# Attention in fp32: the first quarter of the softmax weights split into two parts like the rest, and a new order for GpSimd's low parts

## The chip, the cores and the metric

The kernel runs on one core of a Trainium2 chip. The metric is the time of the whole program in microseconds of device time, as the median over runs. The core has five engines that work through queues of their own: TensorE (PE) for matrix products, with its weight loads (PEld), VectorE (DVE), ScalarE (ACT), GpSimd (POOL) and SyncE (SP), which issues most of the transfers.

## The reference

One layer of an encoder with 2048 positions and 1024 channels, all in float32: a normalization, one input projection, differential attention with four heads, a recurrent group, an output projection and a gated feed-forward network. The change lies in the attention alone:

```python
def block(start):
    qb = lax.dynamic_slice_in_dim(qh, start, Q_BLOCK, axis=1)
    sc = jnp.einsum('bqhcd,bkhcd->bhcqk', qb, kh).astype(jnp.float32) * scale
    dist = jnp.abs(start + jnp.arange(Q_BLOCK)[:, None] - key_pos[None, :]).astype(jnp.float32)
    sc = sc - slopes[:, None, None, None] * dist
    p = jax.nn.softmax(sc, axis=-1)
    w = p[:, :, 0] - lam * p[:, :, 1]
    return jnp.einsum('bhqk,bkhe->bqhe', w, vh)
```

Each head has two score maps (`c` = 0 and 1, of 64 channels each). Their softmaxes are combined into one weight matrix `w` (`lam` is a number learned), and `w` is multiplied by the values. Then each head's output is normalized (`rms_norm(o, subln_g)`).

## The kernel before

The program has four phases, one after the other: input projections and recurrent group, attention (`phase2`), output projection with its normalization, feed-forward network. A product in fp32 is made in one of two ways. Either PE multiplies fp32 operands directly, or both operands are split into a high part (rounded to fp32r) and a low part (what is left, in fp32r), and `mm3` (L80 to L83) adds up three passes: high by high, high by low, low by high.

The attention goes through 64 query tiles of 128 rows (four heads of 16), one to a `step(n, cur)`. Two tiles of a head form a `Pair`, whose products with the values are made together (256 columns). The steps are a pipeline: step n makes the scores of tile n, and in the same step finishes the softmax of tile n-1 (`b1`), transposes the weights of tile n-2 (`b2`), splits the second half of the weights of tile n-3 (`b3`), and multiplies the weights of an older pair by the values (`pv`). Normalization of the outputs follows two and four steps later (`nrm`, `fin`). PE, DVE, ACT and POOL issue exactly in the order in which `step` is written; the tile framework adds the waits. What a tile goes through:

- `scores(hf)`: PE makes half a row of scores (1024 keys) for both maps, into PSUM tiles `sc`, which have two buffers.
- `biased(c, hf)`: DVE adds the distance bias (`strip`) and keeps the running minimum `mn`; the sum goes to SBUF tiles `e` (L453).
- `softmax(c)`: ACT takes the exponential of the 2048 entries of one map (L458), map 0 at the end of step n and map 1 at the beginning of step n+1.
- `ratio`, `combine(hf)`: DVE makes the factor of the second map (L464, L465) and adds the second map times the factor to the first, in two halves (L469). These are the combinations; all their operands are in SBUF.
- `transposed(i)`, i = 0 to 3: PE transposes a quarter of the 2048 columns into a PSUM tile `tp` (two buffers, L475), and ACT copies it to SBUF (L484): quarter 0 into `wTn`, quarter 1 into `wf` (one buffer), quarters 2 and 3 into the halves of `wg` (two buffers).
- `parts(1)`, `parts(2)`: ACT rounds `wf` (and `wg`) to the high part `wTh` (L75) and POOL subtracts that for the low part `wTl` (L78). Those of `wg` are made a step later than its copies.
- `values(part)`: PE multiplies a quarter of the weights by the values. Quarters 1 to 3 go through `mm3`. Quarter 0 is one fp32 product of `wTn` with `vn` (L507), the sum of the two parts of the values, which POOL makes once a head (L416).
- In the step in which a pair's last quarter is done, ACT copies the output to `o` (L514). POOL has small work for its normalization: `osq`, `s` in one step, `rr`, `rb` (twice) in the next.

In `step` the order around the change is:

```python
if b2:
    b2.transposed(0)
    b2.transposed(1)
    b2.parts(1)
if b3:
    b3.parts(2)
```

and behind it values, `ratio` and `combine(0)` of `b1`, the second half of the scores and of the biased sums, `transposed(2)` and `transposed(3)`, softmax 0, more values, and `combine(1)`.

Of the kernel before, what the change touches and what calls it, by code (L numbers as in the profile page):

```python
# [9 lines left out]
F32 = mybir.dt.float32  # L10
F32R = mybir.dt.float32r
F16 = mybir.dt.float16
BF16 = mybir.dt.bfloat16
AF = mybir.ActivationFunctionType
ALU = mybir.AluOpType
# [3 lines left out]
P = 128  # L19
# [3 lines left out]
NT = S // P  # L23
NH = 4
# [18 lines left out]
def encoder_layer(ctx, tc, x, w_qkr, w_v, w_out, w_up, w_down, w_a, w_x, par, lams, g_attn, g_ffn, g_fin, out):  # L43
# [3 lines left out]
    def pool_of(name, **kw):  # L47
        return tc.tile_pool(name=name, reuse_waits="tile", **kw)
# [314 lines left out]
    def phase2(kp):  # L363
        es = ExitStack()
# [3 lines left out]
        qp = es.enter_context(pool_of("aq", bufs=2))  # L368
        lop = es.enter_context(pool_of("al", bufs=2))
        tp_ = es.enter_context(pool_of("at", bufs=2))  # L370
        vp = es.enter_context(pool_of("av", bufs=2))
        ep = es.enter_context(pool_of("ae", bufs=2))
        pre = es.enter_context(pool_of("apre", bufs=1))
        ps_s = es.enter_context(pool_of("ps_s", bufs=2, space=PSUM))
        ps_t = es.enter_context(pool_of("ps_t", bufs=2, space=PSUM))
        ps_v = es.enter_context(pool_of("ps_v", bufs=1, space=PSUM))
        PQ = 2 * P
        NQ = 1

        ones = cp.tile([P, P], F32, name="ones")  # L380
        V.memset(ones, 1.0)
# [28 lines left out]
        def load_values(h, vs):  # L410
            for vt, src in zip(vs, v_d):
                nc.sync.dma_start(vt.bitcast(F32), src[:, h])

        def sum_values(vs):
            vn = vp.tile([P, 4 * NQ, P], F32, name="vn", tag="vn")
            G.tensor_tensor(out=vn, in0=vs[0][:, 0:4 * NQ, :].bitcast(F32), in1=vs[1][:, 0:4 * NQ, :].bitcast(F32), op=ALU.add)  # L416
            vs.append(vn)

        def load_q(h, g):
            qs = []  # L420
# [6 lines left out]
        class Tile:  # L427
# [38 lines left out]

            def combine(self, hf):
                e0, e1 = [e[:, hf * 1024:(hf + 1) * 1024] for e in self.e]
                V.scalar_tensor_tensor(out=e0, in0=e1, scalar=self.rc, in1=e0, op0=ALU.mult, op1=ALU.add)  # L469

            def transposed(self, i):

                tp = ps_t.tile([P, 4, P], F32, name="tp", tag="tp")
                for m in range(4):
                    T.transpose(tp[:, m, :], self.e[0][:, (4 * i + m) * P:(4 * i + m + 1) * P], ident)  # L475
                if i == 0:
                    dst = self.pair.wn[:, :, self.t % 2 * P:(self.t % 2 + 1) * P]
                elif i == 1:
                    dst = self.wf = tp_.tile([P, 4, P], F32, name="wf", tag="wf", bufs=1)
                else:  # L480
                    if i == 2:
                        self.wg = tp_.tile([P, 8, P], F32, name="wg", tag="wg")
                    dst = self.wg[:, (i - 2) * 4:(i - 1) * 4, :]
                A.activation(out=dst, in_=tp, func=AF.Copy)  # L484

            def parts(self, i):

                j = self.t % 2
                dst = (slice(None), slice(0, 4) if i == 1 else slice(4, 12), slice(j * P, (j + 1) * P))
                split(self.pair.wh[dst], self.pair.wl[dst], self.wf if i == 1 else self.wg, lo_eng=G)  # L490

        class Pair:


            def __init__(self, h, u, vs):
                self.h, self.u, self.vs = h, u, vs
                self.s0 = sm.tile([P, 2], F32, name="s0", tag="s0", bufs=8)
                self.wn = hip.tile([P, 4 * NQ, PQ], F32, name="wTn", tag="wTn")
                self.wh = hip.tile([P, NT - 4 * NQ, PQ], F32R, name="wTh", tag="wTh")
                self.wl = lop.tile([P, NT - 4 * NQ, PQ], F32R, name="wTl", tag="wTl")  # L500

            def values(self, part):
                if part == 0:
                    self.pv = ps_v.tile([P, PQ], F32, name="pv", tag="pv")
                for kt in range(part * 4, part * 4 + 4):
                    if part < NQ:
                        T.matmul(self.pv, self.vs[2][:, kt, :], self.wn[:, kt, :], start=kt == 0, stop=False)  # L507
                    else:
                        m = kt - 4 * NQ
                        mm3(self.pv, self.vs[0][:, kt, :], self.vs[1][:, kt, :], self.wh[:, m, :], self.wl[:, m, :],  # L510
                            kt == 0, kt == NT - 1)
                if part == 3:
                    self.o = sm.tile([P, PQ], F32, name="o", tag="o", bufs=3)
                    A.activation(out=self.o, in_=self.pv, func=AF.Copy)  # L514
                    self.sq = sm.tile([P, PQ], F32, name="osq", tag="osq", bufs=1)
                    G.tensor_tensor(out=self.sq, in0=self.o, in1=self.o, op=ALU.mult)
                    self.s2 = sm.tile([P, 2], F32, name="s2", tag="s2")
                    G.tensor_tensor(out=self.s2, in0=self.s0, in1=self.s0, op=ALU.mult)
# [73 lines left out]
        def step(n, cur):  # L592

            b1 = tiles[n - 1] if 0 <= n - 1 < last else None
            b2 = tiles[n - 2] if 0 <= n - 2 < last else None
            pair = lambda lag: pairs[(n - lag) // 2] if n >= lag and (n - lag) // 2 < len(pairs) else None
            pv, nrm, fin = pair(4), pair(6), pair(8)
            if n % 2:
                nrm = fin = None
            b3 = tiles[n - 3] if 0 <= n - 3 < last else None  # L600
            if cur:
                cur.scores(0, n < 3)
            if n < 3:
                keep_clock(nrm_ps[:, 0:P], 3)
            if b1:
                b1.softmax(1)
            if cur:
                cur.biased(0, 0)
                cur.biased(1, 0)
            if b2:  # L610
                b2.transposed(0)
                b2.transposed(1)
                b2.parts(1)
            if b3:
                b3.parts(2)
            if pv:
                pv.values(n % 2 * 2)
            if fin:
                fin.norm_spread()
            if b1:  # L620
                b1.ratio()
                b1.combine(0)
            if cur:
                cur.scores(1, n < 3)
                if n < 3:
                    keep_clock(nrm_ps[:, 0:P], 3)
                cur.biased(0, 1)
                cur.biased(1, 1)
            if b2:
                b2.transposed(2)  # L630
                b2.transposed(3)
            if cur:
                cur.softmax(0)
            if pv:
                pv.values(n % 2 * 2 + 1)
            if nrm:
                nrm.norm_sums()
            if b1:
                b1.combine(1)
            if fin:  # L640
                fin.scaled()
            if nrm:
                nrm.norm_scale()

        ordered = {mybir.EngineType.PE, mybir.EngineType.DVE, mybir.EngineType.Activation, mybir.EngineType.Pool}
        ks, vs = load_head(0, [slice(0, D)])
# [7 lines left out]
        qs_next = load_q(0, 0)  # L654
        load_keys(0, ks, [slice(D, S)])
        load_values(0, vs)
        sum_values(vs)
        n = 0
        manual = ExitStack()
        manual.enter_context(tc.manual_schedule(engines=ordered))  # L660
# [1 line left out]
        for h in range(NH):  # L662
            for t in range(NT):
# [6 lines left out]
                if t % 4 == 1:  # L670
                    if t + 4 < NT:
                        qs_next = load_q(h, t // 4 + 1)
                    elif h + 1 < NH:
                        nxt = load_head(h + 1, [slice(0, S)])
                        qs_next = load_q(h + 1, 0)
                        load_values(h + 1, nxt[1])
                if t == NT - 1 and h + 1 < NH:
                    sum_values(nxt[1])
                if h == NH - 1 and t in (6, 8, 10, 12):
                    raw = fetch_out(t // 2 + 1)  # L680
                if h == NH - 1 and t in (7, 9, 11, 13):
# [823 lines left out]
```

## Time and profile before

| | us |
|---|---|
| median of three runs | 2653.01 (2652.57 to 2661.96) |
| the profiled execution, its own time | 2648.49 |
| its span, first to last instruction | 2646.7 |
| PE busy | 2583.5 (98%) |
| DVE busy | 1976.1 (75%) |
| ACT busy | 1341.9 (51%) |
| POOL busy | 586.3 (22%) |

The shares are over the whole span. Attention is one phase of four, so its limits are read from windows inside it and from the timeline of a step, not from these shares. The ends of PE's matrix products are modelled, so that PE may look busy while it waits; waits are better read from the idle times in brackets at the ends of timeline rows.

### The profile page before, as it was taken

To read this page: it belongs to the slowest core of one execution; us is meant where nothing else is said; L and a number is where in the kernel's file an instruction comes from. 1 tells how busy PE (TensorE), PEld (TensorE's weight loads), DVE (VectorE), ACT (ScalarE), POOL (GpSimd) and SP (SyncE) were. 2 spreads that over 40 slices of the span, in tenths; PEclk is the share of its full clock that TensorE was granted. 3 is DMA by queue.
4 is the path that set the end of the run, shared out by engine and by line. 5 is a ranking of instruction groups with operands and counts; after the bars stand their busy time and mean duration, and the time that the engine had idled before them with its cause. 6 is when DMAs were issued, how large, how long until landed. Compare 5 with 4: busy or idle time off the path is not lost. (4 is left out here: it accounts for less than half of the span.)

```text
span 2646.7 us, 33694 instructions
## 1 busy us (share of the span) xinstructions
PE 2583.5 (98%) x13018; PEld 2107.9 (80%) x13018; DVE 1976.1 (75%) x2487; ACT 1341.9 (51%) x1732; POOL 586.3 (22%) x488
## 2 busy tenths in 40 slices
PE   9999999999999999999999999989999999999998
PEld 7878778778888888787778888878888887778786
DVE  5454554699999999644488888898888777675776
ACT  4343542688888888632344444454444443332433
POOL 0113313346667676700000000000000000111100
PEclk9999999999999999999999999999999999999999
DMA  6421221321202001344443343454665344755743
GB/s 192 132 88 58 82 80 64 133 93 34 72 23 88 25 25 39 99 152 136 173 158 131 131 147 120 151 162 157 242 227 203 128 147 116 210 121 131 233 148 128
DMA packets 146018, 329.36 MB, mean 124 GB/s; under 512 B 18624, under 2 KB 74688, under 8 KB 137024
## 3 DMA queue, kind: packets, MB, share of 16 engines
q1 hardware_dynamic: 133632, 283.82, 31.1%
q0 software_dynamic: 11504, 41.42, 6.4%
q8 instruction: 102, 1.67, 0.3%
q10 hardware_dynamic: 720, 1.95, 0.2%
q14 instruction: 60, 0.49, 0.1%
HBM read 198.16 MB, written 128.97 MB: 124 GB/s over the span
## 5 line engine op out<-in xcount | busy, mean ns | idle before, releaser
L1003 ACT ACTIVATE wg<-sw 128x1024 fp32r<-128x1024 f32 (+1 forms) x136 | 140.7, 1034 | 399.3 <-PE q L1029 220.6
L1044 DVE TENSOR_TENSOR u<-q,u 128x512 f32<-128x512 f32 x340 | 234.3, 689 | 138.8 <-PE q L1029 134.9
L458 ACT ACTIVATE e<-e,mn 128x2048 f32<-128x2048 f32 x128 | 256.2, 2007 | 11.3 <-DVE mn L453 11.3
L449 PE MATMUL sc<-ks,qt 64*128 64x512 f32 x1536 | 228.2, 410 | 6.2 <-DVE mn L453 6.0
L1189 DVE SCALAR_TENSOR_TENSOR acc<-u,prm,acc 128x1023 f32<-128x1023 f32 (+1 forms) x176 | 225.9, 1284 | 8.5 <-ACT acc L1181 4.0
L469 DVE SCALAR_TENSOR_TENSOR e<-e,rc,e 128x1024 f32<-128x1024 f32 x128 | 211.1, 1650 | 2.3
L83 PE MATMUL ps<-hT_hi,wl 128*128 128x512 f32 x512 | 199.6, 390 | 0.0
L82 PE MATMUL ps<-hT_lo,wh 128*128 128x512 f32 x512 | 199.6, 390 | 0.0
L81 PE MATMUL ps<-hT_hi,wh 128*128 128x512 f32 x512 | 199.4, 390 | 0.0
L449 PEld LDWEIGHTS sc<-ks,qt 64*128 64x128 f32 x1536 | 147.5, 184 | 45.2 <-DVE mn L453 9.3
L1008 DVE TENSOR_TENSOR wg<-sw,wg 128x1024 fp32r<-128x1024 f32 (+1 forms) x136 | 161.7, 1189 | 28.0 <-ACT wg L1003 28.0
L1008 DVE TENSOR_TENSOR wg<-wr,wg 128x512 fp32r<-128x512 f32 (+3 forms) x136 | 126.8, 932 | 68.3 <-ACT wg L1003 68.3
L1003 ACT ACTIVATE wg<-wr 128x512 fp32r<-128x512 f32 (+3 forms) x136 | 111.7, 822 | 118.9 <-PE q L1029 104.9
L453 DVE CUSTOM_DVE_ANT_0 e<-sc,strip,mn 128x1024 f32<-128x1024 f32 x128 | 159.1, 1280 | 14.2 <-PE sc L449 13.3
L1294 POOL DMA_DIRECT2D b15f<-in_w_down_dram x1 | 0.8, 814 | 705.0 <-DVE u L1102 705.0
L78 POOL TENSOR_TENSOR wTl<-wg,wTh 128x1024 fp32r<-128x1024 f32 x64 | 156.5, 2446 | 0.0
L453 DVE CUSTOM_DVE_ANT_0 e<-sc,strip 128x1024 f32<-128x1024 f32 x128 | 150.8, 1213 | 5.0 <-PE sc L449 5.0
L1029 PE MATMUL q<-b0r,wg 128*128 128x512 f32 x448 | 152.7, 398 | 0.0
L1029 PE MATMUL q<-b14r,wg 128*128 128x512 f32 x440 | 149.4, 397 | 2.9 <-ACT u L1051 2.9
L78 POOL TENSOR_TENSOR wTl<-wf,wTh 128x512 fp32r<-128x512 f32 x64 | 126.7, 1980 | 110.1 <-ACT wTh L75 107.4
L1029 PE MATMUL q<-b12r,wg 128*128 128x512 f32 x440 | 149.4, 397 | 0.0
L475 PEld LDWEIGHTS tp<-ident,e 128*128 128x128 f32 x1024 | 110.6, 141 | 45.2 <-ACT wTh L75 18.7
(320 smaller groups left out, 6669.6 us busy)
## 6 DMA issues: line engine op xcount, KB each, us to landing
wr<-in_w_up_dram SPq DMA_DIRECT2D x66, 512.0 KB, 5.5
s_d<-sw SPq DMA_DIRECT2D x22, 1024.0 KB, 4.7
sw<-s_d SPq DMA_DIRECT2D x22, 1024.0 KB, 4.8
a_d<-acc SPq DMA_DIRECT2D x154, 128.0 KB, 1.9
x_d<-u POOLq DMA_DIRECT2D x32, 512.0 KB, 5.4
wr<-a_d SPq DMA_DIRECT2D x32, 512.0 KB, 4.8
xt<-in_x_dram SPq DMA_DIRECT2D x30, 512.0 KB, 4.6
ws<-in_w_qkr_dram SPq DMA_DIRECT2D x16, 512.0 KB, 3.3
```

The lines of the kernel that those rows point to most:

```text
L78: lo_eng.tensor_tensor(out=lo, in0=src, in1=hi, op=ALU.subtract)
L82: T.matmul(ps, lh, rl, start=False, stop=False)
L83: T.matmul(ps, ll, rh, start=False, stop=last)
L449: T.matmul(self.sc[c][:, n * CH:(n + 1) * CH], l[rows, q], r[rows, kk], start=i == 0, stop=i == 2)
L453: V.tensor_tensor_reduce(out=self.e[c][:, hf * 1024:(hf + 1) * 1024], in0=self.sc[c], in1=strip[:, off:off + 1024], scale=SLOPES[self.h], ...
L458: A.activation(out=self.e[c], in_=self.e[c], func=AF.Exp, scale=-1.0, bias=self.mn[:, 2 * c + 1:2 * c + 2], accum_out=self.s[c])
L469: V.scalar_tensor_tensor(out=e0, in0=e1, scalar=self.rc, in1=e0, op0=ALU.mult, op1=ALU.add)
L1003: A.activation(out=hi, in_=src, func=AF.Copy)
L1008: V.tensor_tensor(out=lo, in0=src, in1=hi, op=ALU.subtract)
L1029: T.matmul(ps, l, r[:, k, :], start=new is not None and k == 0 and n == 0, stop=k == m - 1 and n == 2, skip_group_check=True)
L1044: V.tensor_tensor(out=out, in0=a, in1=b_, op=ALU.add)
L1189: V.scalar_tensor_tensor(out=acc[:, 0:n], in0=u[:, o + tap:o + tap + n], scalar=prm[:, C_FW + 3 * m + tap:C_FW + 3 * m + tap + 1], in1=acc ...
```

## The change

The first quarter is now treated like the others. `transposed(0)` no longer copies `tp`: ACT rounds it from PSUM into the high part, and DVE subtracts that from PSUM for the low part. `wTh` and `wTl` hold all 16 blocks of keys, `wTn`, `vn` and `sum_values` are gone, and `values` always uses `mm3`. The tile `wg` has one buffer in place of two. In `step`, `parts(2)` of `b3` now stands ahead of `parts(1)` of `b2`, which moved behind `combine(0)`. Two dependencies are added by hand: POOL's low part of `wg` waits for the `combine(1)` of the step before, its low part of `wf` for the `combine(0)` of the same step.

```diff
             def combine(self, hf):
                 e0, e1 = [e[:, hf * 1024:(hf + 1) * 1024] for e in self.e]
-                V.scalar_tensor_tensor(out=e0, in0=e1, scalar=self.rc, in1=e0, op0=ALU.mult, op1=ALU.add)
+                return V.scalar_tensor_tensor(out=e0, in0=e1, scalar=self.rc, in1=e0, op0=ALU.mult, op1=ALU.add)
...
                 if i == 0:
-                    dst = self.pair.wn[:, :, self.t % 2 * P:(self.t % 2 + 1) * P]
+
+                    o = (slice(None), slice(0, 4), slice(self.t % 2 * P, (self.t % 2 + 1) * P))
+                    A.activation(out=self.pair.wh[o], in_=tp, func=AF.Copy)
+                    V.tensor_tensor(out=self.pair.wl[o], in0=tp, in1=self.pair.wh[o], op=ALU.subtract)
+                    return
                 elif i == 1:
                     dst = self.wf = tp_.tile([P, 4, P], F32, name="wf", tag="wf", bufs=1)
                 else:
                     if i == 2:
-                        self.wg = tp_.tile([P, 8, P], F32, name="wg", tag="wg")
+                        self.wg = tp_.tile([P, 8, P], F32, name="wg", tag="wg", bufs=1)
                     dst = self.wg[:, (i - 2) * 4:(i - 1) * 4, :]
                 A.activation(out=dst, in_=tp, func=AF.Copy)
 
             def parts(self, i):
 
                 j = self.t % 2
-                dst = (slice(None), slice(0, 4) if i == 1 else slice(4, 12), slice(j * P, (j + 1) * P))
-                split(self.pair.wh[dst], self.pair.wl[dst], self.wf if i == 1 else self.wg, lo_eng=G)
+                dst = (slice(None), slice(4, 8) if i == 1 else slice(8, 16), slice(j * P, (j + 1) * P))
+                src = self.wf if i == 1 else self.wg
+                A.activation(out=self.pair.wh[dst], in_=src, func=AF.Copy)
+                return G.tensor_tensor(out=self.pair.wl[dst], in0=src, in1=self.pair.wh[dst], op=ALU.subtract)
...
                 for kt in range(part * 4, part * 4 + 4):
-                    if part < NQ:
-                        T.matmul(self.pv, self.vs[2][:, kt, :], self.wn[:, kt, :], start=kt == 0, stop=False)
-                    else:
-                        m = kt - 4 * NQ
-                        mm3(self.pv, self.vs[0][:, kt, :], self.vs[1][:, kt, :], self.wh[:, m, :], self.wl[:, m, :],
-                            kt == 0, kt == NT - 1)
+                    mm3(self.pv, self.vs[0][:, kt, :], self.vs[1][:, kt, :], self.wh[:, kt, :], self.wl[:, kt, :],
+                        kt == 0, kt == NT - 1)
...
             if b2:
                 b2.transposed(0)
                 b2.transposed(1)
-                b2.parts(1)
             if b3:
-                b3.parts(2)
+                after(b3.parts(2), "second")
...
             if b1:
                 b1.ratio()
-                b1.combine(0)
+                marks["first"] = b1.combine(0)
+            if b2:
+                after(b2.parts(1), "first")
...
             if b1:
-                b1.combine(1)
+                marks["second"] = b1.combine(1)
...
+        def after(ins, mark):
+
+            if mark in marks:
+                tc.add_manual_dep(ins.ins, marks[mark].ins.name,
+                                  mybir.DependencyInfo(mybir.DependencyClass.Sync, mybir.DependencyReason.SCHED_ONLY),
+                                  reason="shared access to SBUF")
```

On ACT, a step from the middle of the attention stood so before; a number in a name is that of a tile, `wg_7757` and `wg_7865` are the `wg` of two tiles that follow each other, and `tp` are the transposes:

```order
L484 ACTIVATE wTn_7470<-tp_7811 128x4x128
L484 ACTIVATE wf_7822<-tp_7817 128x512
L75 ACTIVATE wTh_7471<-wf_7822 128x4x128
L75 ACTIVATE wTh_7471<-wg_7757 128x8x128
L484 ACTIVATE wg_7865<-tp_7860 128x512
L484 ACTIVATE wg_7865<-tp_7867 128x512
```

A step of the change on ACT, between the same neighbours:

```order
L472 ACTIVATE wTh_7605<-tp_7963 128x4x128
L481 ACTIVATE wf_7975<-tp_7970 128x512
L488 ACTIVATE wTh_7605<-wg_7909 128x8x128
L488 ACTIVATE wTh_7605<-wf_7975 128x4x128
L481 ACTIVATE wg_8018<-tp_8013 128x512
L481 ACTIVATE wg_8018<-tp_8020 128x512
```

The first copy became a high part, and the high part of `wg` moved ahead of that of `wf`. The copies into the next `wg` stand behind both, as before.

On POOL, two steps of the attention before, the second with the small work `rr` and `rb`:

```order
L78 TENSOR_TENSOR wTl_5130<-wf_5478,wTh_5129 128x4x128
L78 TENSOR_TENSOR wTl_5130<-wg_5413,wTh_5129 128x8x128
L516 TENSOR_TENSOR osq_5544<-o_5542 128x256
L518 TENSOR_TENSOR s2_5546<-s0_4905 128x2
L78 TENSOR_TENSOR wTl_5342<-wf_5589,wTh_5341 128x4x128
L78 TENSOR_TENSOR wTl_5130<-wg_5521,wTh_5129 128x8x128
```

and of the change:

```order
L489 TENSOR_TENSOR wTl_5169<-wg_5468,wTh_5168 128x8x128
L489 TENSOR_TENSOR wTl_5169<-wf_5534,wTh_5168 128x4x128
L510 TENSOR_TENSOR osq_5600<-o_5598 128x256
L512 TENSOR_TENSOR s2_5602<-s0_4936 128x2
L489 TENSOR_TENSOR wTl_5169<-wg_5577,wTh_5168 128x8x128
L489 TENSOR_TENSOR wTl_5388<-wf_5645,wTh_5387 128x4x128
```

The low part of `wg` moved ahead of that of `wf` in every step.

On DVE, a step of the change from the biased sums of its first half of the scores (L446, an instruction and the reading of its accumulator) to the last combination (L462):

```order
L446 ISA e_5612,mn<-sc,strip 128x1024
L446 ISA mn 128x1
L446 ISA e_5613,mn<-sc,strip 128x1024
L446 ISA mn 128x1
L473 TENSOR_TENSOR wTl<-tp,wTh 128x4x128
L457 RECIPROCAL rc<-s_5504 128x1
L458 SCALAR_TENSOR_TENSOR rc<-rc,s_5386,nlam 128x1
```

Only the row of L473 is new; before, the reciprocal followed the biased sums directly.

## Rows read from the trace of the kernel before

**Rows 1.** Windows: us, busy PE, PEld, DVE, ACT, POOL, granted clock, DMA share, GB/s.

```profile
550.00:560.00 10.00, 8.47 (x45) 6.29 (x43) 9.73 (x13) 9.47 (x13) 4.97 (x3) 0.83 0.18 54
...
700.00:800.00 100.00, 100.00 (x760) 84.00 (x758) 96.73 (x150) 87.81 (x119) 69.52 (x52) 1.00 0.10 30
```

**Rows 2.** Instructions on the score tiles: ns min/median/max, first and last start in us.

```profile
L449 PE MATMUL sc<-ks,qt x1536: 383/393/504, 522.0 to 1083.6; 64*128 64x512 f32 x192
```

**Rows 3.** Waits from 570 to 1080 us: who for whom, total us, times, longest.

```profile
POOL wTl L78 <- ACT wTh L75: 87.2, 57, 5.4
ACT wg L484 <- PE tp L475: 52.3, 53, 1.4
...
ACT wg L484 <- POOL wTl L78: 2.0, 3, 1.1
```

**Rows 4.** Timeline of ACT: start, length, instruction, idle time before it.

```profile
868.92 2.02 ACT L458 ACTIVATE e<-e,mn 128x2048 f32<-128x2048 f32 x1
...
871.17 2.02 ACT L458 ACTIVATE e<-e,mn 128x2048 f32<-128x2048 f32 x1
...
873.15 0.61 ACT L484 ACTIVATE wTn<-tp 128x512 f32<-128x512 f32 x1
...
874.28 0.63 ACT L75 ACTIVATE wTh<-wf 128x512 fp32r<-128x512 f32 x1
874.82 1.04 ACT L75 ACTIVATE wTh<-wg 128x1024 fp32r<-128x1024 f32 x1
876.80 1.09 ACT L484 ACTIVATE wg<-tp 128x512 f32<-128x512 f32 x2 [0.93 <-PE tp L475]
877.77 2.01 ACT L458 ACTIVATE e<-e,mn 128x2048 f32<-128x2048 f32 x1
```

**Rows 5.** Timeline of POOL.

```profile
868.29 2.43 POOL L78 TENSOR_TENSOR wTl<-wg,wTh 128x1024 fp32r<-128x1024 f32 x1
...
874.99 1.89 POOL L78 TENSOR_TENSOR wTl<-wf,wTh 128x512 fp32r<-128x512 f32 x1 [2.56 <-ACT wTh L75]
876.84 2.41 POOL L78 TENSOR_TENSOR wTl<-wg,wTh 128x1024 fp32r<-128x1024 f32 x1
```

**Rows 6.** Timeline of DVE.

```profile
865.91 1.28 DVE L469 SCALAR_TENSOR_TENSOR e<-e,rc,e 128x1024 f32<-128x1024 f32 x1
...
869.52 2.28 DVE L469 SCALAR_TENSOR_TENSOR e<-e,rc,e 128x1024 f32<-128x1024 f32 x1
...
874.01 0.15 DVE L464 RECIPROCAL rc<-s 128x1 f32<-128x1 f32 x1
...
874.45 1.28 DVE L469 SCALAR_TENSOR_TENSOR e<-e,rc,e 128x1024 f32<-128x1024 f32 x1
...
878.57 1.76 DVE L469 SCALAR_TENSOR_TENSOR e<-e,rc,e 128x1024 f32<-128x1024 f32 x1
```

**Rows 7.** Groups of POOL by line and form: busy us, mean ns.

```profile
L416 POOL TENSOR_TENSOR vn<-vt 128x512 f32<-128x512 f32 x3 | 3.8, 1277 | 0.0
```

**Rows 8.** Timeline of PE.

```profile
872.18 1.89 PE L507 MATMUL pv<-wTn,vn 128*128 128x256 f32 x8
873.91 0.61 PE L539 MATMUL nrm_ps<-ident,rb 128*128 128x128 f32 x4
...
876.89 0.37 PE L81 MATMUL pv<-wTh,vt 128*128 128x256 f32 x1
...
878.40 0.50 PE L523 MATMUL nrm_ps<-ones,osq 128*128 128x2 f32 x4
```

**Rows 9.** Timeline of DVE in the value projection of the first phase.

```profile
106.25 0.68 DVE L78 TENSOR_TENSOR vl<-ps,vh 128x512 fp32r<-128x512 f32 x1
106.85 0.68 DVE L77 CAST wh<-ws 128x1024 fp32r<-128x1024 f32 x1
```

**Rows 10.** Timeline of PE in the first steps of the attention.

```profile
552.46 0.49 PE L449 MATMUL sc<-ks,qt 64*128 64x512 f32 x1 [0.82 <-DVE mn L453]
...
557.02 2.69 PE L507 MATMUL pv<-wTn,vn 128*128 128x256 f32 x8
```

More of the change, by code (lines that the diff above doesn't have):

```diff
@@ L370, in phase2 @@
         tp_ = es.enter_context(pool_of("at", bufs=2))
-        vp = es.enter_context(pool_of("av", bufs=2))
         ep = es.enter_context(pool_of("ae", bufs=2))
@@ L377, in phase2 @@
         PQ = 2 * P
-        NQ = 1
         ones = cp.tile([P, P], F32, name="ones")
@@ L412, in load_values @@
                 nc.sync.dma_start(vt.bitcast(F32), src[:, h])
[L414 to L417, printed above, removed]
         def load_q(h, g):
@@ L497, in __init__ @@
                 self.s0 = sm.tile([P, 2], F32, name="s0", tag="s0", bufs=8)
-                self.wn = hip.tile([P, 4 * NQ, PQ], F32, name="wTn", tag="wTn")
-                self.wh = hip.tile([P, NT - 4 * NQ, PQ], F32R, name="wTh", tag="wTh")
-                self.wl = lop.tile([P, NT - 4 * NQ, PQ], F32R, name="wTl", tag="wTl")
+                self.wh = hip.tile([P, NT, PQ], F32R, name="wTh", tag="wTh")
+                self.wl = lop.tile([P, NT, PQ], F32R, name="wTl", tag="wTl")
             def values(self, part):
@@ L643, in step @@
                 nrm.norm_scale()
+        marks = {}
+        def after(ins, mark):
[3 more added lines that the diff above has]
+                                  reason="shared access to SBUF")
         ordered = {mybir.EngineType.PE, mybir.EngineType.DVE, mybir.EngineType.Activation, mybir.EngineType.Pool}
@@ L656, in phase2 @@
         load_values(0, vs)
-        sum_values(vs)
         n = 0
@@ L676, in phase2 @@
                         load_values(h + 1, nxt[1])
-                if t == NT - 1 and h + 1 < NH:
-                    sum_values(nxt[1])
                 if h == NH - 1 and t in (6, 8, 10, 12):
```

## The prediction

> **What bounds the kernel now.** I read the windows first: in the attention phase PE is recorded as busy all the time and DVE for 97% of it, with ACT at 88% and POOL at 70% [rows 1]. PE's ends are modelled, so I turned to the times of the score products. They run from 522.0 to 1083.6 us [rows 2], and that is 64 steps (four heads of sixteen query tiles), so a step takes 561.6/64 = 8.78 us. What each engine waits for tells who paces whom: ACT waits for transposes (52.3 us over 53 of some 58 steps, 0.99 us each) and nearly never for POOL (2.0 us in all); POOL waits for ACT (87.2 us) [rows 3]. So ACT has about a microsecond to spare in a step, POOL more, and PE and DVE set the pace together.
>
> The timeline of ACT shows one step in order of issue: softmax 0, (every second step the copy of the output `o`), softmax 1, the copy `wTn`, the copy `wf`, the high parts `wTh<-wf` and `wTh<-wg`, then the two copies into `wg`, and again softmax 0 [rows 4]. The idle microsecond lies before the copies into `wg`, and its end is a transpose of PE, not POOL.
>
> POOL and DVE show the second thing to see. A combination that meets no low part takes 1.28 us; the one at 869.52 us, issued while POOL was in the `wg` low part of 868.29 us (2.43 us long), takes 2.28 us [rows 5, 6]. It goes the other way too: the `wf` low part at 874.99 us began while DVE was in the combination of 874.45 to 875.73 us, and took 1.89 us [rows 5, 6], where a POOL sum of the same 128x512 form (`vn`) has 1.28 us [rows 7]. Of the 1.89 us, 0.74 us went by before the combination ended and 1.15 us after. So whichever of the two starts second waits for the first. The change is aimed at the longer combinations, and it can only gain what they lose: in the two steps around 865 to 880 us that is 0, 1.0, 0 and about 0.5 us.
>
> **The change, part by part.**
>
> *PE.* The first quarter's eight fp32 records take 1.73 us up to the next group (872.18 to 873.91); twelve three-pass records take 1.51 us (876.89 to 878.40) [rows 8]. That saves 0.2 us in every second step, nothing in the others.
>
> *DVE.* One subtraction from PSUM per step is added, `wTl<-tp`, 128x512 to fp32r with one PSUM operand. The same form stands in the value projection: 0.60 us from its start to the next one's (106.25 to 106.85) [rows 9]. In exchange the combinations could lose up to 0.75 us in a step. By itself this is a draw, worth about 0.1 us a step.
>
> *ACT.* Copy `wTn` is replaced by the high part `wTh<-tp` of the same size, priced at the same 0.61 us. The high part of `wg` now stands ahead of that of `wf`. Both are the same work as before.
>
> *POOL.* Its low parts swap: `wg` first, then `wf`. The four sums `vn` go (4 x 1.28 us, behind other work). The added waits cost nothing: the `wg` low part waits for the second combination of the step before, which is past by then, and the `wf` low part for a combination that ends before the `wg` low part has begun.
>
> *The buffer.* `wg` now has one buffer where it had two. This is the part that I think decides. The copies into `wg` (tile n-2) in a step must now wait until POOL's low part of the `wg` of tile n-3 **in the same step** has read the buffer; with two buffers they waited for the one of the step before. On ACT, in order, everything that follows waits too: softmax 0, softmax 1, `wTh<-tp`, `wf`, `wTh<-wg`. And the next `wg` low part waits for the last of these. That closes a ring through ACT and POOL, once a step.
>
> Its length, laid out on the times of ACT's row group [rows 4], for a step with the copy of `o`: softmax 0 starts at 868.92, softmax 1 at 871.17, the first copy at 873.15 (ends 873.76), and `wf` behind it. The instruction after `wf` starts at 874.28; it is now `wTh<-wg`, 1.04 us, to 875.32. From the end of an ACT instruction to the POOL one that waits for it is 0.08 us (874.28 + 0.63 = 874.91 to 874.99) [rows 4, 5], so POOL could begin at 875.40. Meanwhile DVE: it is released by `wTh<-tp` at 873.76 + 0.08 = 873.84, subtracts for 0.60 us to 874.44, needs 0.44 us for the ratio (874.01 to 874.45) [rows 6], and starts the first combination at 874.88, half a microsecond ahead of POOL. It ends at 876.16 with POOL waiting. After it POOL needs 2.43 us less the 0.13 us that the held-up `wf` low part was shorter after the release (1.28 - 1.15): 878.46. ACT goes on at 878.54; from the first copy into `wg` to softmax 0 is 0.97 us (876.80 to 877.77) [rows 4]: 879.51. The ring is 879.51 - 868.92 = 10.59 us; without `o` softmax 1 follows 1.98 us after softmax 0 (as the copy at 873.15 follows softmax 1) and not 2.25, so 10.32 us. The mean is 10.46 us against 8.78: **1.68 us a step more**.
>
> [...]
>
> Can the others follow at 10.46 us? DVE's work in a step is 8.78 us at most now; with the subtraction (0.60 us) and, if the second combination always meets the `wf` low part, another 1.0 us, it is at most 10.38 us, even if none of today's collisions goes away. PE's is 8.78 us at most. Both wait then, and the gains named above (PE's 0.2 us, DVE's 0.1 us) disappear in their waits.
>
> The first `wg` low part is in step 3, so 61 steps count: 61 x 1.68 = 102 us. The profiled execution took 2648.5 us, 1.8 of them outside its span of 2646.7; with 102 us it is 2751. The median of the runs shown is 4.5 us above it, so I put the change at 2653 + 102 = **2755 us**.
>
> **The rivals.**
>
> *The ring is there, but POOL is not held by the first combination* (DVE comes late, or both run side by side). Then POOL starts at 875.40 and ends at 877.83: 0.63 us a step less, so +64 us, 2717 us. For it speaks only that the two starts lie half a microsecond apart; against it, that DVE has nothing else to do before them.
>
> *The buffer wait does not bite, and the kernel is no slower.* For that the `wg` low part would have to be over when the transposes are done, at 876.80 on the same scale [rows 4], 1.66 us earlier than I find. Then PE's 17.5 us for two steps, less 0.2 us, would set the pace: 31 x 0.2 = 6 us, 2647 us. It decides where POOL's low part and the hold before it shrink from 3.1 to 1.4 us together; the shortest 128x1024 low part in the timeline takes 2.4 us [rows 5], so I give it little.
>
> [...]
> [...]
>
> *DVE is late as well.* If the second combination is always held by the `wf` low part and this delays the next step's subtraction, a step grows towards 11 us: +135 us, 2788 us.
>
> **How the numbers follow.** The ring with POOL held has 76% (2735 to 2775 us: 0.3 us a step either way for the terms that no row shows, the subtraction's and high part's strided targets and the wake-up of ACT). The ring with POOL not held has 10% (2705 to 2730). DVE late as well 5% (2775 to 2800), the clock 3% (above 2800), no slower 6% (2640 to 2655). A range from 2705 to 2785 us leaves out the last two and part of the third. 0.5% of 2653 us is 13 us, about what a measurement here can tell from no change: slower 0.94, within it 0.04, faster 0.02.
>
> **What would show it.** In the changed profile ACT's copies into `wg` wait some 2.7 us a step for POOL's low part (875.87, the end of `wTh<-wf` on the scale above, to 878.54) instead of a microsecond for PE; score products span some 660 us in place of 562; PE and DVE each show a wait in every step; first combinations take 1.28 us and POOL's `wg` low parts about 3.1 us. It is wrong if those copies still wait for PE, if the `wg` low part begins before the first combination, or if the granted clock in the phase is below 1.

## The result and the profile after

The changed kernel takes **2749.2 us** (median of four runs, 2748.46 to 2753.86); the kernel before took 2655.4 us (2652.57 to 2661.96) on the same chip. The ratio is 1.0359 [1.0345, 1.0372]: 94 us slower. The profiled execution took 2753.86 us.

The page's first part (span, then busy time, share and instructions of PE) and the row of the score tiles over the attention phase (count, shortest, median and longest ns, first and last start):

```profile
span 2752.1 us, 34103 instructions
...
PE 2624.8 (95%) x13146; PEld 2119.7 (77%) x13146; DVE 2025.6 (74%) x2551; ACT 1334.2 (48%) x1732; POOL 575.6 (21%) x484
```

```profile
L442 PE MATMUL sc<-ks,qt x1536: 383/393/792, 523.3 to 1182.3; 64*128 64x512 f32 x192
```

The span of the profiled execution grew by 105.4 us (the two profiled executions lie further apart than the medians), and the stretch in which scores are made by 659.0 - 561.6 = 97.4 us of these [rows 2]. 659.0/64 is 10.30 us a step. The waits from 590 to 1170 us (waiting engine, tile and line; what ended the wait; sum, count, longest):

```profile
ACT wg L481 <- POOL wTl L489: 153.5, 56, 2.8
POOL wTl L489 <- ACT wTh L488: 141.8, 55, 3.1
PEld sc L442 <- DVE mn L446: 70.7, 95, 1.0
...
DVE wTl L473 <- ACT wTh L472: 46.4, 52, 1.3
```

Before, ACT waited 2.0 us for POOL in the whole phase [rows 3]; now it waits 153.5/56 = 2.7 us in each step, and POOL waits 2.6 us for ACT. Two engines that wait for each other once a step, both for longer than anything else does, are the mark of a ring: each can go on only when the other is done. It can be walked on the timelines (start, duration, engine, line, operation; idle time before and what ended it). ACT, one step and the beginnings of the next two:

```profile
861.49 2.01 ACT L451 ACTIVATE e<-e,mn 128x2048 f32<-128x2048 f32 x1
...
863.48 2.00 ACT L451 ACTIVATE e<-e,mn 128x2048 f32<-128x2048 f32 x1
...
865.46 0.59 ACT L472 ACTIVATE wTh<-tp 128x512 fp32r<-128x512 f32 x1
865.94 0.60 ACT L481 ACTIVATE wf<-tp 128x512 f32<-128x512 f32 x1
866.42 1.07 ACT L488 ACTIVATE wTh<-wg 128x1024 fp32r<-128x1024 f32 x1
867.37 0.64 ACT L488 ACTIVATE wTh<-wf 128x512 fp32r<-128x512 f32 x1
870.71 1.08 ACT L481 ACTIVATE wg<-tp 128x512 f32<-128x512 f32 x2 [2.70 <-POOL wTl L489]
871.68 2.00 ACT L451 ACTIVATE e<-e,mn 128x2048 f32<-128x2048 f32 x1
...
882.23 2.01 ACT L451 ACTIVATE e<-e,mn 128x2048 f32<-128x2048 f32 x1
```

DVE in the same step, with the added subtraction and the two combinations:

```profile
866.09 0.69 DVE L473 TENSOR_TENSOR wTl<-tp,wTh 128x512 fp32r<-128x512 f32 x1 [0.52 <-ACT wTh L472]
...
867.14 1.29 DVE L462 SCALAR_TENSOR_TENSOR e<-e,rc,e 128x1024 f32<-128x1024 f32 x1
...
870.75 2.26 DVE L462 SCALAR_TENSOR_TENSOR e<-e,rc,e 128x1024 f32<-128x1024 f32 x1
```

POOL:

```profile
867.57 3.10 POOL L489 TENSOR_TENSOR wTl<-wg,wTh 128x1024 fp32r<-128x1024 f32 x1 [2.20 <-ACT wTh L488]
870.64 1.28 POOL L489 TENSOR_TENSOR wTl<-wf,wTh 128x512 fp32r<-128x512 f32 x1
```

From softmax 0 to softmax 0 it is 871.68 - 861.49 = 10.19 us without the copy of `o` (10.32 predicted) and 882.23 - 871.68 = 10.55 us with it (10.59 predicted). The first of the two is made of softmax 0 (1.99 us to the next), softmax 1 (1.98), 1.68 us until the first combination starts, its 1.29, 2.24 us until POOL's low part is over (870.67), 0.04 until ACT starts, and 0.97 us of copies. POOL could have begun at 867.57 but was held until 868.43.

The windows (length; busy us and count of PE, PEld, DVE, ACT, POOL; granted clock, DMA share, GB/s) and PE's pauses in the step:

```profile
700.00:800.00 100.00, 90.41 (x659) 72.06 (x657) 90.45 (x134) 72.58 (x102) 55.55 (x42) 1.00 0.11 38
```

```profile
869.68 0.49 PE L442 MATMUL sc<-ks,qt 64*128 64x512 f32 x1
870.89 1.66 PE L442 MATMUL sc<-ks,qt 64*128 64x512 f32 x11 [0.71 <-DVE mn L446]
```

No engine is full any more [rows 1], and the clock is still 1.00, with PE pausing in every step.

### The profile page after: what moved, and what is told of

Same layout as the page of the kernel before. It is cut to its first block, busy times and chain, and to the rows that moved or that the text cites. A ratio compares the mean times of both kernels' runs of the same rounds, so it can differ in the third digit from the quotient of the medians.

```text
span 2752.1 us, 34103 instructions
## 1 busy us (share of the span) xinstructions
PE 2624.8 (95%) x13146; PEld 2119.7 (77%) x13146; DVE 2025.6 (74%) x2551; ACT 1334.2 (48%) x1732; POOL 575.6 (21%) x484
## 5 line engine op out<-in xcount | busy, mean ns | idle before, releaser
L442 PE MATMUL sc<-ks,qt 64*128 64x512 f32 x1536 | 266.1, 419 | 50.5 <-DVE mn L446 50.4
L442 PEld LDWEIGHTS sc<-ks,qt 64*128 64x128 f32 x1536 | 157.5, 186 | 117.4 <-DVE mn L446 82.4
L489 POOL TENSOR_TENSOR wTl<-wg,wTh 128x1024 fp32r<-128x1024 f32 x64 | 198.2, 3097 | 167.5 <-ACT wTh L488 164.3
L462 DVE SCALAR_TENSOR_TENSOR e<-e,rc,e 128x1024 f32<-128x1024 f32 x128 | 225.3, 1760 | 2.3
L81 PE MATMUL pv<-wTh,vt 128*128 128x256 f32 x512 | 155.6, 304 | 17.4 <-ACT o L508 17.4
L446 DVE CUSTOM_DVE_ANT_0 e<-sc,strip,mn 128x1024 f32<-128x1024 f32 x128 | 159.0, 1280 | 1.7 <-issue 1.5
L446 DVE CUSTOM_DVE_ANT_0 e<-sc,strip 128x1024 f32<-128x1024 f32 x128 | 150.8, 1213 | 5.9 <-PE sc L442 3.6
L481 ACT ACTIVATE wg<-tp 128x512 f32<-128x512 f32 x128 | 69.6, 596 | 174.4 <-POOL wTl L489 172.2
```

The source lines that it names most:

```text
L81: T.matmul(ps, lh, rh, start=first, stop=False)
L442: T.matmul(self.sc[c][:, n * CH:(n + 1) * CH], l[rows, q], r[rows, kk], start=i == 0, stop=i == 2)
L446: V.tensor_tensor_reduce(out=self.e[c][:, hf * 1024:(hf + 1) * 1024], in0=self.sc[c], in1=strip[:, off:off + 1024], scale=SLOPES[self.h], ...
L462: return V.scalar_tensor_tensor(out=e0, in0=e1, scalar=self.rc, in1=e0, op0=ALU.mult, op1=ALU.add)
```

## The experiments

Times are medians; ratios are to the kernel before, run on the same chip. A pace is read from the score products recorded from 600 to 1000 us, 24 a step; they come in groups of 12, so a window's edges leave it uncertain by about 1%. For the kernel before (the score line's windows: length, PE, PEld, clock, DMA, GB/s) and for the change:

```profile
600.00:1000.00 400.00, 157.07 (x1094) 101.03 (x1092) 1.00 0.14 44
```

```profile
600.00:1000.00 400.00, 156.89 (x924) 91.45 (x924) 1.00 0.12 40
```

That is 400 x 24/1094 = 8.78 us a step, and 10.39 us.

### Is it the buffer?

**before_one_wg**: the kernel before, with only this edit.

```diff
-self.wg = tp_.tile([P, 8, P], F32, name="wg", tag="wg")
+self.wg = tp_.tile([P, 8, P], F32, name="wg", tag="wg", bufs=1)
```

> The kernel before with one buffer for wg and nothing else. Theory: the same ring closes, through both low parts in the order of before: from softmax 0 to the end of the wg high part 6.9 us, the wf low part until 7.35, the wg low part until 9.8, the copies and softmax 0 again at 10.85 us with the copy of o, 10.6 without; 1.9 us a step over 61 steps, about 2770 us, with ACT waiting for POOL some 2.5 us a step. Rival (the loss comes from the subtraction on DVE or from the new order of the low parts, not from the buffer): 2655 us.

2771.6 us, 1.0429 [1.0412, 1.0446], as expected. One buffer alone costs more than the whole change, by the same wait (590 to 1150 us; the second row and the window with all engines are used below):

```profile
ACT wg L484 <- POOL wTl L78: 149.2, 53, 2.9
...
PE pv L507 <- ACT o L514: 41.4, 26, 1.6
```

```profile
600.00:1000.00 400.00, 354.82 (x2481) 284.23 (x2483) 324.93 (x492) 292.40 (x397) 190.72 (x172) 0.98 0.12 40
```

**no_added_waits**: the change without its two added dependencies.

```diff
-            if mark in marks:
+            if False:
```

> The change without its two hand-made dependencies. Theory: both are over by the time POOL gets there, so nothing moves: 2749 us within 5. Rival: the waits hold POOL back and are part of the loss; then some tens of us faster, with POOL's wg low part starting earlier in the step.

2749.6 us, 1.0349 [1.0333, 1.0364]: the change's own time. The added waits cost nothing and order nothing that the ring doesn't.

**no_first_combine**: leaves out the combination that holds POOL, and with it the added wait for it.

```diff
-                marks["first"] = b1.combine(0)
```

> The change with the first combination left out (the first 1024 keys of the weights are then those of the first map alone). Theory: POOL's wg low part is not held behind the first combination, so the ring is shorter by that hold, 0.7 us a step, and the low part takes 2.4 us in place of 3.1: about 40 us less, 2708 us. Rival (DVE is the bound, the ring only seems to be): the whole 1.2 us of the combination come off each step, 75 us less, 2675 us. Second rival (ACT and PE alone set the step): no change, 2749 us.

2699.4 us, 1.0162 [1.0147, 1.0178], and 998 score products, 9.62 us a step. The low part of `wg` runs in the time that it takes alone (600 to 1000 us; shortest, median, longest ns):

```profile
L489 POOL TENSOR_TENSOR wTl<-wg,wTh x42: 2395/2412/2442, 600.2 to 995.1; 128x1024 fp32r<-128x1024 f32 x42
```

So the first combination is a link of the ring and worth 50 us.

**two_wg**: the change with its second buffer back; `ch0` gives up its own place for it and stands in a buffer of `e0` that is free by then.

```diff
-self.wg = tp_.tile([P, 8, P], F32, name="wg", tag="wg", bufs=1)
+self.wg = tp_.tile([P, 8, P], F32, name="wg", tag="wg", bufs=2)
```

> The change with two buffers for wg again (room for the second is made by placing one tile of the tail, ch0, in a buffer of e0 that is free by then). Theory: the ring through ACT and POOL is open, ACT's copies into wg wait for PE as before and no longer for POOL. The step then depends on DVE: POOL's wg low part starts about 4.2 us after the last biased sum of the step before, ahead of the first combination (4.8 us), which is held until 6.6 and ends at 7.6; with two biased sums (2.4 us) behind it the step is about 10.0 us, so the kernel lands near 2727 us, 20 to 25 us below the change. Rival: the single buffer is the whole loss, the low parts' new order costs nothing; then the step is that of before, 2650 to 2660 us. Second rival: the buffer is not the cause at all; 2749 us and ACT waiting for POOL as in the change.

2770.3 us, 1.0427 [1.0409, 1.0445]. The first theory had it right that the ring opens and that the first combination is then held, but it gave 10.0 us a step and 2727 us; both rivals failed. The ring is gone (ACT waits for PE's transposes again, 590 to 1150 us), and yet a step takes 400 x 24/894 = 10.74 us:

```profile
ACT wg L480 <- PE tp L467: 81.8, 52, 2.7
```

```profile
600.00:1000.00 400.00, 151.81 (x894) 93.89 (x896) 0.92 0.12 40
```

A step of it with a held combination, on POOL, DVE and PE:

```profile
868.35 2.39 POOL L488 TENSOR_TENSOR wTl<-wg,wTh 128x1024 fp32r<-128x1024 f32 x1 [1.40 <-ACT wTh L487]
```

```profile
868.43 3.39 DVE L461 SCALAR_TENSOR_TENSOR e<-e,rc,e 128x1024 f32<-128x1024 f32 x1
```

```profile
873.07 0.49 PE L441 MATMUL sc<-ks,qt 64*128 64x512 f32 x1 [1.46 <-DVE mn L445]
874.28 2.93 PE L441 MATMUL sc<-ks,qt 64*128 64x512 f32 x11 [0.71 <-DVE mn L445]
```

POOL begins 0.08 us ahead of the first combination, and now it is DVE that is held: 3.39 us for 1.28. The biased sums behind it are late, PE stands for 1.46 and 0.71 us, the granted clock falls to 0.92, and eleven score products take 2.93 us where the change has 1.66. This is not so in every step. Of the 37 first combinations from 600 to 1000 us 19 take 3.38 to 3.49 us and the others 1.28 or 1.29; the median of all is as without a hold (count, shortest, median, longest ns):

```profile
L461 DVE SCALAR_TENSOR_TENSOR e<-e,rc,e x74: 1272/1285/3493, 600.9 to 995.2; 128x1024 f32<-128x1024 f32 x74
```

From the first combination at 858.22 us, which takes 1.28 us, to the next at 868.43 us a step still takes 10.21 us; DVE waits there for score products in its turn (1.20 us before its next sum, and 36.0 us over 39 waits in the window). So behind the ring a second loss lies hidden, and the hold is only one part of it.

### What is behind the ring?

**three_pass_only**: the three passes alone, with the order of the kernel before, two buffers (as in two_wg, not shown) and no added waits.

```diff
                 b2.transposed(1)
+                b2.parts(1)
             if b3:
-                after(b3.parts(2), "second")
+                b3.parts(2)
...
-            if b2:
-                after(b2.parts(1), "first")
```

> The first quarter in three passes with the low parts in the order of before (wf, then wg), no added waits, two buffers for wg. Theory: no ring, ACT's copies into wg wait for PE; POOL's low parts meet the combinations as before; only DVE's subtraction of 0.6 us is new, and since DVE has about 0.25 us a step to spare, the step grows by 0.35 to 0.6 us: 2677 to 2692 us. Rival (the new order costs nothing once there are two buffers): as the run with two buffers, 2770 us. Second rival (the subtraction is paid by fewer collisions): 2655 us.

2804.2 us, 1.0572 [1.0555, 1.0588]: all expectations missed, and the slowest of all. The score line's window (11.43 us a step), the same window with all engines, then DVE, POOL and PE in one step with a held combination:

```profile
600.00:1000.00 400.00, 146.10 (x840) 91.64 (x840) 0.89 0.11 38
```

```profile
600.00:1000.00 400.00, 351.07 (x2399) 293.24 (x2400) 351.10 (x492) 276.93 (x370) 188.84 (x156) 0.89 0.11 38
```

```profile
864.87 0.68 DVE L472 TENSOR_TENSOR wTl<-tp,wTh 128x512 fp32r<-128x512 f32 x1
...
866.21 3.38 DVE L461 SCALAR_TENSOR_TENSOR e<-e,rc,e 128x1024 f32<-128x1024 f32 x1
```

```profile
864.86 1.30 POOL L488 TENSOR_TENSOR wTl<-wf,wTh 128x512 fp32r<-128x512 f32 x1
866.11 2.39 POOL L488 TENSOR_TENSOR wTl<-wg,wTh 128x1024 fp32r<-128x1024 f32 x1
```

```profile
870.85 0.50 PE L441 MATMUL sc<-ks,qt 64*128 64x512 f32 x1 [1.71 <-DVE mn L445]
...
874.26 1.97 PE L467 MATMUL tp<-ident,e 128*128 128x128 f32 x8
```

In the kernel before, the first combination was over before POOL's `wg` low part began (865.91 + 1.28 against 868.29) [rows 5, 6]. Now the subtraction stands ahead of it on DVE; in the step shown it comes 0.10 us behind POOL and is held for 2.1 us, as it is in 17 of the 35 steps from 600 to 1000 us. The pauses of PE are longer than in two_wg (up to 2.5 us) and the clock lower; eight transposes take 1.97 us where the change has 1.09.

**three_pass_late**: the same, with the subtraction issued behind the first combination and the second quarter transposed first, so that `tp` can wait for it.

```diff
-                    V.tensor_tensor(out=self.pair.wl[o], in0=tp, in1=self.pair.wh[o], op=ALU.subtract)
+                    self.first = (o, tp)
...
             if b2:
-                b2.transposed(0)
                 b2.transposed(1)
+                b2.transposed(0)
...
                 marks["first"] = b1.combine(0)
+            if b2:
+                o, tp = b2.first
+                V.tensor_tensor(out=b2.pair.wl[o], in0=tp, in1=b2.pair.wh[o], op=ALU.subtract)
```

> As the run with three passes alone (low parts in the order of before, two buffers for wg), but DVE's subtraction stands behind the first combination, and the second quarter is transposed ahead of the first. Theory: it was not the 0.6 us of the subtraction but its place that cost 150 us: ahead of the ratio it makes the first combination late, POOL's two low parts get in front of it, PE stands still long enough for its clock to fall. Behind the combination none of this happens; what is left is DVE's 0.6 us where about 0.25 is spare: 2665 to 2700 us, granted clock 1.00, first combinations about 1.3 us. Rival (the work itself, or the transposes that wait for the subtraction, is the cost): 2750 us or more.

2659.0 us, 1.0019 [1.0009, 1.0028], 8.82 us a step at clock 1.00:

```profile
600.00:1000.00 400.00, 161.00 (x1088) 104.62 (x1084) 1.00 0.13 44
```

The same work in another place on DVE: 145 us between this kernel and three_pass_only. (The two edits, subtraction and transposes, were made together and not apart.)

**after_late**: the change itself, one buffer, with the same edit of the subtraction.

> The change itself, one buffer for wg, with DVE's subtraction behind the first combination. Theory: the ring stays, but the first combination starts 0.6 us earlier and holds POOL's wg low part 0.1 in place of 0.7 us: 37 us less than the change, 2712 us, and ACT still waits for POOL some 2 us a step. Rival (the ring only follows DVE's pace): the step falls to that of DVE, 2680 us or less, or nothing changes.

2700.8 us, 1.0174 [1.0158, 1.019]: 9.54 us a step (1006 score products), 11 us less than expected. The first combination is over before POOL begins; what is left is the bare ring (`wTl` from 600 to 1000 us; waits from 590 to 1070):

```profile
L489 POOL TENSOR_TENSOR wTl<-wg,wTh x42: 2394/2407/2425, 601.2 to 995.9; 128x1024 fp32r<-128x1024 f32 x42
```

```profile
ACT wg L481 <- POOL wTl L489: 96.2, 48, 2.0
```

**two_wg_late**: both mended, the second buffer of two_wg and the subtraction of three_pass_late; the new order and the added waits stay.

> The change with both of its expensive places mended: two buffers for wg, and DVE's subtraction behind the first combination; the new order of the low parts and the added waits stay. Theory: the ring is open and the first combination starts ahead of the wg low part, so neither loss of the two is left; the second combination meets the wf low part and takes about 2.1 us, 0.4 us more than in the run with three passes and the late subtraction: 2660 to 2690 us, granted clock 1.00. Rival (the new order is a loss of its own, as the run with two buffers alone could be read): 2740 us or more.

2662.4 us, 1.0031 [1.002, 1.0042]; 400 x 24/1092 = 8.79 us a step:

```profile
600.00:1000.00 400.00, 161.84 (x1092) 105.43 (x1092) 1.00 0.13 44
```

Second combinations take 1.5 to 1.7 us, not the 2.1 expected. POOL's `wg` low part is still held here (3.01 us in the median of the same window); without the ring that costs the step nothing that can be seen.

**three_pass_filled**: is it the pauses, or the clock that falls with them? three_pass_only, with twenty more passes for PE in each pair.

```diff
+                    if kt in (7, 15):
+                        for _ in range(10):
+                            T.matmul(self.pv, self.vs[0][:, kt - 1, :], self.wh[:, kt - 1, :], start=False, stop=False)
```

> As the run with three passes alone, with ten more passes of one block in the second group of value products of every step (each 0.117 us, so 1.2 us more work for PE a step; the output counts that block several times). It asks how much of that run's loss is the fallen clock. If most of it is, PE at work keeps its clock and the kernel gets faster although it does more, 2740 to 2790 us at a granted clock of 0.97 or more. If the clock is only a by-product, the time stays or grows, 2804 to 2870 us.

2796.0 us, 1.0528 [1.0503, 1.0554]. All engines from 600 to 1000 us, and PE's longest waits (590 to 1070 us):

```profile
600.00:1000.00 400.00, 374.49 (x2812) 322.11 (x2809) 360.07 (x504) 284.27 (x379) 196.52 (x162) 0.96 0.12 40
```

```profile
PE sc L441 <- DVE mn L445: 31.1, 44, 0.8
```

The clock rose from 0.89 to 0.96 and the time fell by 8 us (the intervals of the two ratios barely miss each other) although PE had more to do. That lies between the two expectations and speaks for the lower clock as a part of that loss. How large a part, an estimate from the rows of three_pass_only can only bound: its 840/24 = 35 steps would take 307 of the 400 us at the pace of before, so 93 us are lost. PE stood for 400 - 351 = 49 us, and the mean clock of 0.89 takes at most 0.11 x 400 = 44 us of work from it directly. What a slow group of PE delays in its turn is not in that.

### Was there anything to gain?

In these three the low parts really stand behind the combinations. ACT makes the high part of `wg` right after softmax 0, so that POOL has it early; POOL's `wg` low part is issued first in the next step, its small work behind that, and its `wf` low part behind the first combination. `wg` has one buffer.

```diff
+                b2.parts(1, "high")
             if b3:
-                after(b3.parts(2), "second")
+                after(b3.parts(2, "low"), "second")
...
             if b2:
-                after(b2.parts(1), "first")
+                after(b2.parts(1, "low"), "first")
...
+            if b2:
+                b2.parts(2, "high")
```

**behind_early** is the change in that order.

> The change with its low parts really behind the combinations: ACT makes the wg high part right after softmax 0 of the same step, so that POOL's wg low part can start as the second combination ends; the small work of POOL (osq, rr, rb) moves behind it; one buffer for wg. Theory: the ring is then softmax 0, high part, low part, copies, about 6.5 us, and no longer binds; combinations take 1.28 us. But softmax 1 and the high part of the first quarter come about a microsecond later, so DVE waits for that high part some 0.5 us a step: between 2650 and 2690 us. Rival (one buffer for wg binds whatever the order): 2740 us or more.

2693.2 us, 1.015 [1.0136, 1.0163]: slower than the expected range. From 600 to 1000 us all combinations take 1275 to 1286 ns, so none is held, but a step takes 9.27 us (1036 score products). DVE waits 0.6 us a step for the high part of the first quarter (25.1 us over 43), as foreseen; what else makes the step no run took apart.

**behind_late** has the late subtraction as well.

> As the run before it, and DVE's subtraction for the first quarter moves behind the first combination (the second quarter is transposed first). Theory: DVE no longer waits for the high part, no combination meets a low part, PE alone sets the step at 8.65 us: 2647 us, 0.3% faster than before. Rival (three passes cost DVE more than the collisions did): 2665 us or more.

2676.8 us, 1.0088 [1.0074, 1.0102]: the time lies in the rival's range, and its reason was not tested. From 560 to 960 us a step takes 9.0 us (1066 score products); now PE's transposes wait for the `tp` that the late subtraction still reads (590 to 1080 us):

```profile
PEld tp L468 <- DVE wTl L630: 22.3, 52, 3.1
```

**before_behind** is the kernel before (fp32 first quarter) in that order.

> The first quarter as in the kernel before (one fp32 product), with the order of the two runs before it: wg high part after softmax 0, wg low part behind the second combination, wf low part behind the first, one buffer for wg. Theory: DVE loses the collisions and has no subtraction, so PE sets the step at about 8.7 us: 2650 us, 0.2% faster than before or the same. It shows what of the run before it is owed to the order and what to the three passes.

2670.7 us, 1.0061 [1.0048, 1.0073], a little slower than expected. It answers the question best. Its combinations from 560 to 960 us (busy us, mean ns, idle before), then its score line:

```profile
L469 DVE SCALAR_TENSOR_TENSOR e<-e,rc,e 128x1024 f32<-128x1024 f32 x92 | 128.0, 1392 | 1.6
```

```profile
560.00:960.00 400.00, 158.29 (x1104) 109.61 (x1104) 1.00 0.13 44
```

In the kernel before, the same two rows are:

```profile
L469 DVE SCALAR_TENSOR_TENSOR e<-e,rc,e 128x1024 f32<-128x1024 f32 x91 | 150.0, 1649 | 1.6
```

```profile
560.00:960.00 400.00, 158.43 (x1104) 102.46 (x1100) 1.00 0.13 43
```

DVE got 22 us back in 400, and the pace didn't move: 8.70 us a step in both. What DVE got back it spent in part on waiting: for score products 65 times in the phase in place of 36 (30.5 us in place of 18.3). The collisions at which the change aims were covered by PE. In its last head POOL also splits weights for the next phase, and there combinations are still held (one takes 3.37 us at 1016.42). Its last score product starts at 1096.3 us, 12.7 us later than before [rows 2], all of it lost in that stretch, where the granted clock falls as well (the score line's windows of this run and of the kernel before):

```profile
1040.00:1080.00 40.00, 15.10 (x84) 9.66 (x84) 0.87 0.07 26
```

```profile
1040.00:1080.00 40.00, 16.18 (x108) 10.36 (x108) 1.00 0.12 37
```

No run took this apart.

## Why the prediction was right, and where a step of it was wrong

The four kernels that carry the new order (us):

| | subtraction ahead of the first combination | behind it (and the transposes swapped) |
|---|---|---|
| one `wg` buffer | 2749.2 (the change) | 2700.8 |
| two `wg` buffers | 2770.3 | 2662.4 |

**The ring: right, in place and size.** 10.19 and 10.55 us for 10.32 and 10.59; 10.39 against 8.78 us over 400 us is +1.61 a step for +1.68, and 61 steps of it are 98 us, for 97.4 us of longer score time. What was too long: the low part takes 2.24 us after the release where I took 2.30, and ACT starts 0.04 us after it where I took 0.08. That `wTh<-wg` starts 0.48 us after `wf` and not 0.65 changes nothing, since POOL then only waits longer for the combination.

**POOL held by the first combination: right.** 3.10 us at 867.57, of which 0.86 before the release; no_first_combine takes 50 us off. The rival without the hold (2717 us, 38 below the forecast) came out as 2699 to 2701, 48 to 50 below the change, where the hold was really taken away (no_first_combine, after_late). The low part is 0.71 us shorter there (median 3120 ns in the change from 600 to 1000 us, 2407 in after_late) where I took 0.63; 61 x 0.71 = 43 us, and no run took the rest apart.

**The added waits at nothing: right** (no_added_waits). **DVE late as well: not so.** The second combination does meet the `wf` low part (2.26 us at 870.75), but the next subtractions still wait for ACT, 0.9 us each (46.4 us over 52), so this is covered.

**The clock: right for the change; beside it, it fell.** In the change PE pauses for 0.3 to 0.7 us between groups, step after step, and the clock is 1.00. In two_wg and three_pass_only, with pauses of up to 1.5 and 2.5 us, it fell to 0.92 and 0.89, and from 550 to 560 us of the kernel before it was 0.83, with one of 0.82 us [rows 1, 10]. The length of a pause does not sort the runs, though: from 600 to 1000 us three_pass_filled has a clock of 0.96 with no pause over 0.8 us, and before_one_wg 0.98 with one of 1.6 us in every second step. What made the clock fall is not shown. That a fall of the clock leads above 2800 us was the author's estimate, and no row shows where it comes from: of the four runs with a clock below 1 in that window one took more (2804 us), the others 2770 to 2796 us.

**The step that failed** is the one on DVE: "By itself this is a draw, worth about 0.1 us a step", and with it the price of the rival in which the buffer wait does not bite, 2647 us. I counted the subtraction's 0.6 us, and not what it delays: the first combination, which before was through ahead of POOL's `wg` low part and now, in about every second step, comes just behind it (0.1 us in the steps shown); the sums behind it are late, PE pauses (1.46 and 0.71 us in the step shown of two_wg) and its clock is lower (0.92 in two_wg, 0.89 in three_pass_only). Measured without the ring (two_wg) that rival gives 2770 us, and with the old order as well (three_pass_only) 2804 us. That the place is to blame and not the work, the runs with the late subtraction show, but for the swapped transposes, which no run parts from it; how the loss divides among the hold, the pauses and the clock is not shown. The total hid all this: under the ring POOL's low part is late itself, DVE comes first, and the hold falls to POOL. On this term the forecast held by luck, because the ring was there. The ring is not "the cause" of 94 us in the sense that mending it gives them back: mended alone it makes things worse by 21 us, the subtraction alone gives 48, both together 87.

**"PE and DVE set the pace together": not so.** In before_behind DVE lost 22 us of combinations in 400 at the same pace, so DVE was not what set it.

**PE's 0.2 us in every second step: not seen.** three_pass_late and two_wg_late, where both losses are gone, run at 8.82 and 8.79 us a step, for 8.78. DVE is busy for 394.5 to 394.7 of 400 us there, so whether it hides PE's gain is open. No version here beat the kernel before.

## What to carry to other kernels

A tile with one buffer, written by one in-order engine and read by another that waits for a later instruction of the first, closes a ring: its length can be summed from a timeline before the change is built (here 10.32 and 10.59 us a step, and 10.19 and 10.55 were measured). An instruction that is put ahead of one which another engine can hold (here a combination of 3.39 us for 1.28) is to be priced by who comes first afterwards, not by its own duration. And before collisions are removed, look whether anything waits for the engine that loses time in them: here 22 us in 400 could be given back to DVE without the pace noticing.

## What the runs showed that was not expected

- A tenth of a microsecond can decide who is held. In two_wg POOL starts at 868.35 and DVE at 868.43, and DVE's combination takes 3.39 us; in the change DVE has 0.43 us of lead, and POOL's low part takes 3.10 us for 2.41. What is held takes a little less after the release than alone: 2.24 us for 2.41 (the low part in the change) and 1.08 us (870.74 to 871.82) for 1.28 (the combination in two_wg).
- At a lower clock the same work of PE takes longer. In the kernel before eight transposes take 1.09 us at 550.55, at a granted clock of 1.00, and 1.97 us at 555.26, where it is 0.50 (555.3 to 557.0 us): 1.8 times as long. In two_wg, at 0.92 in the mean, eleven score products behind a pause were seen at 2.93 us for 1.66, 1.8 times as long too; the clock in those 2.93 us is not shown. With the additional passes for PE in three_pass_filled the mean clock is 0.96 and not 0.89, so some of it comes back, and no more than that.
